# Sixteen of 24 modulation steps of the second layer in the even layer's last part, paced by product columns; ten small transfers of the odd layer on GpSimd's queue

## The chip, the core and the metric

The kernel runs on one core of a Trainium2 chip. The time is what the device takes for one execution, in microseconds (us). An execution on one core has a few engines that run side by side, each with its own queue of instructions: TensorE (PE, with PEld for its weight loads), VectorE (DVE), ScalarE (ACT), GpSimd (POOL) and SyncE (SP). SP computes nothing here; it issues DMA transfers. GpSimd issues some too. Engines wait for each other and for transfers by semaphores.

## The reference

A trunk of two layers over a prompt of 1024 tokens and 8 sample tokens (1032 columns in the kernel), width 1024. Each layer has a token mixer and an MLP, and each of these takes six vectors (shift, scale and gate, twice) from a small product of the condition `c` with a big matrix:

```python
for l in range(DEPTH):
    mod = jax.nn.silu(c) @ ada_w[l] + ada_b[l]      # (.., 1024) @ (1024, 6144)
    sh1, s1, g1, sh2, s2, g2 = split(mod, 6)
    h = rmsnorm(x, norm_mix[l]) * (1 + s1) + sh1
    x = x + g1 * mixer_l(h)        # l = 0: HGRN2 heads and gated short convolutions; l = 1: Mamba-2 (SSD)
    h = rmsnorm(x, norm_mlp[l]) * (1 + s2) + sh2
    x = x + g2 * (relu(h @ w1) ** 2 @ w2)
y = rmsnorm(x, norm_final)
```

(shortened: the prompt and the samples have their own `c`, nine columns together, and the mixers are not shown.) The matrix `ada_w[l]` is 1024 x 6144 in float32, 25.2 MB for each layer. Nothing but `c` goes in, so layer 1's `mod` can be computed at any time before layer 1 reads it.

The odd layer's mixer needs, for each half of the prompt, step sizes `dt` of 32 heads, their running sums times A, the exponentials of these, and for the sample tokens `dt` and `exp(dt*A)` spread to all channels of a head.

## The kernel before

The kernel goes through the program in stages, in this order: even layer (its last part about 350 to 512 us of the span, and a closing GEMM to 542), first MLP with a pass A to about 890 and a pass B to about 1270, odd layer to 2110, second MLP with pass A to 2437 and pass B to 2811. Products of float32 are made of three products of a rounded part and a remainder (`mm3`, lines 484, 487 and 488: high with high, high with low, low with high).

**Weights.** They come in units of 128 x 1024 on SP's queue (`raw<-W`), are rounded by ScalarE (`whi`) and the remainder is taken by VectorE (`wlo`). `need` takes the next unit from a list and prepares units up to three ahead (`AHEAD`). The transfers that SP issues stay in program order, so whatever stands in front of a weight tile on that queue, and waits, holds it up.

**Modulation.** `ada_gen(l, alloc, groups, depth)` is a generator. `groups` lists blocks of 512 columns by number (0 and 1 are the first shift, and so on to 11). One step is a quad: four products of 32 x 512 (line 316) that run side by side on quarters of the array, plus four loads of 256 KB each for the step `depth` ahead. A group of four blocks takes 8 quads, one of two blocks 4; then ScalarE copies the sums, TensorE transposes them (line 328) and VectorE adds the bias into `mod`. The accumulator stays taken from the group's first quad to the copy. `ada_steps(n)` makes n steps, and `need` calls it with `ada_rate`, one step for each weight unit.

**Where its steps stand before.** In the even layer's last part layer 0's groups (6, 7, 8, 9) and (10, 11) run, 12 quads, one for each weight unit. In the first MLP's pass B all 24 quads of layer 1 run, from unit 9 of 64 on, one for each unit. Pass B keeps four accumulators (`pd`) in PSUM, from which the modulation takes its own. Its units are the list `BOPS`; line 953 adds an accumulator, times a gate, into `x`, and the sample sums `racc` are added at line 960.

**Background.** `Background.tick` is called all through the layers and interleaves small pieces of mixer work with the products.

**The odd layer's step sizes.** For each half (hf 0 and hf 1) VectorE and ScalarE compute them, write them to DRAM and read them back spread over partitions. All of it goes by `dma`, that is by SP's queue in program order: running sums (`csd`) and their exponentials (`esd`) out; the last column out (`cdd`) and back as a 128 x 128 tile (`hs`, which must wait until `cdd` has landed); in the first half also the sample tokens' values out (`sd`, two transfers) and back as `dts` (four transfers). `dma_aux` does the same on GpSimd's queue, where the MLPs already issue theirs. In the listing the calls stand in the function that ends with `rest`.

Of the kernel before, what the change touches and what calls it, by code (L numbers as in the profile page):

```python
# [14 lines left out]
P = 128  # L15
# [3 lines left out]
NS = 8  # L19
# [112 lines left out]
class Background:  # L132


    def __init__(self):
        self.gens = []
        self.width, self.rate, self.due = 2, 1.0, 0.0

    def add(self, g, first=False):
        self.gens.insert(0 if first else len(self.gens), g)  # L140
        return g
# [4 lines left out]

    def tick(self, n=1):

        self.due += n * self.rate
        while self.due >= 1.0:  # L150
            self.due -= 1.0
            for g in self.gens[:self.width]:
                self.step(g)
# [8 lines left out]
def kernel(ctx: ExitStack, tc: tile.TileContext, A: dict):  # L162
# [53 lines left out]
    def dma(out, in_):  # L216
        ins = nc.sync.dma_start(out=out, in_=in_)
        if pinned_sp[0]:
            tc.keep_in_program_order(ins)

    def dma_aux(out, in_):

        tc.keep_in_program_order(nc.gpsimd.dma_start(out=out, in_=in_))

    bg = Background()
# [61 lines left out]
    def ada_gen(l, alloc, groups, depth=1, alloc2=None):  # L287
# [21 lines left out]
        for g, ch in enumerate(groups):  # L309
# [35 lines left out]
                V.tensor_add(out, pv[:, 1, :, :, 0:9], tmp)  # L345
            yield

    ada, ada_rate = [iter(())], [1]

    def ada_steps(n):  # L350
        for _ in range(n):
            next(ada[0], None)

    def mi(l, comp):
        return l * 48 + comp * 8
# [114 lines left out]
    def need(kind, idx):  # L470

        i = wpos[0]
        assert order[i] == (kind, idx), (i, order[i], kind, idx)
        wpos[0] += 1
        ada_steps(ada_rate[0])
        while len(units) <= min(i + AHEAD, max(i, limit[0] - 1)):
            units.append(prep(*order[len(units)]))
        u, units[i] = units[i], None
        return u

    def mm3(pt, trip, first=True, last=True):
        n = len(trip)
        for i, (wh, wl, xh, xl) in enumerate(trip):
            mm = PE.matmul(pt, wh, xh, start=first and i == 0, stop=False)  # L484
            if pinned[0]:
                tc.keep_in_program_order(mm)
            PE.matmul(pt, wh, xl, start=False, stop=False)  # L487
            PE.matmul(pt, wl, xh, start=False, stop=last and i == n - 1)  # L488
# [178 lines left out]
    def rows(units):  # L667

        return lambda m: [(hi[:, m * P:m * P + P], lo[:, m * P:m * P + P]) for hi, lo in units]
# [108 lines left out]
    def mlp(l, gi, finish, more=None):  # L778
# [77 lines left out]
        for i, (p, q) in enumerate(AOPS):  # L856
            n = APOS[p, q]
# [70 lines left out]
        for n, (i, hb, q, mp) in enumerate(BOPS):  # L928
            j = n % 8
            hi, lo = need(f"b{l}", n)  # L930
            if n == 8 and more:
                ada[0] = more()
            elif i == 6 and hb == 0 and j == 0:
                ada_steps(99)
            rh, rl = R[i, q // 2]
            seq = BSEQ if i else BFIRST
            qs = [qq for qq, mm in seq if mm == mp]
            for m in (2 * mp, 2 * mp + 1):
                if q == qs[0]:
                    pts[m] = pd()  # L940
                pt = pts[m]
                for b in range(2) if hb is None else (hb,):
                    c = slice(b * hw, b * hw + hw)
                    mm3(pt[:, b, 0:hw], [(hi[:, o:o + P], lo[:, o:o + P], rh[:, k, c], rl[:, k, c])
                                         for k, o in ((q % 2 * 4 + k, 256 * k + m % 2 * P) for k in range(4))],
                        q == qs[0], q == qs[-1])
                if q == qs[-1]:
                    for o, th in BOUT[BPROD[i]]:
                        mt = 4 * o + m
                        gate = mod[:, gi + mt, 0:1]  # L950
                        if hb is None:
                            xv = v2(x[:, mt, th * HX:th * HX + HX])
                            V.scalar_tensor_tensor(xv, pt[:, :, 0:hw], gate, xv, op0=ALU.mult, op1=ALU.add)  # L953
                        else:
                            xv = x[:, mt, th * HX + hb * hw:th * HX + hb * hw + hw]
                            V.scalar_tensor_tensor(xv, pt[:, hb, 0:hw], gate, xv, op0=ALU.mult, op1=ALU.add)
                        if hb != 1:
                            sv = pt[:, 0, 0:4] if th else pt[:, 1, hw - 4:hw]
                            av = acc[:, mt, 4 * th:4 * th + 4]
                            V.tensor_add(av, sv, av)  # L960

            if i == 0:
                split_op((2, 2, 2, 2, 0, 1, 2, 1)[j])
            else:
                split_op((0, 0, 1, 1, 1, 1, 0, 1)[j] if i == 1 else (2, 1, 1, 1, 1, 1, 0, 1)[j] if i < 6 else (2, 1, 0, 0, 0, 0, 0, 0)[j] if hb == 0 else 0)
            if j == (5 if i else 3) and i < 6:
                load_op(i + 1, 1)
            elif j == 7 and i < 5:
                load_op(i + 2, 0)

            if i == 6 and j == 7 and hb == 0:
                V.tensor_mul(acc, acc, mod[:, gi:gi + KT, 1:9])
                for k in FOURS:
                    V.tensor_add(x[:, k, 512:520], acc[:, k], xs[:, k])
            if i >= 5:
                next(fin, None)
            bg.tick()
# [316 lines left out]
    def even_mixer(res, last, rest):  # L1294
        hgrn_consts()
        V.tensor_scalar(gnh, vec("gn"), -0.5, None, op0=ALU.mult)
        dma(scs, A["st_sc"])
        fa = [new_ff(), new_ff()]
        g01 = head(0, fa[0], rest, fa[1])
        g01 += head(1, fa[1])  # L1300
        fb = [new_ff(), new_ff()]
        g23 = head(2, fb[0])
        bg.drain(*g01)
        out_seq(rows([need("eo", 0), need("eo", 1)]), [ff_src(f) for f in fa], res)
        g23 += head(3, fb[1])
        c0 = conv_uv(0)
        c1 = conv_uv(1)
        bg.drain(*g23)
        ada_steps(99)
        turn = [0]  # L1310

        def alloc(w):
            turn[0] += 1
            return t2(w) if turn[0] % 2 else t3(w)
        ada[0] = ada_gen(0, alloc, ((6, 7, 8, 9), (10, 11)))
        out_seq(rows([need("eo", 2), need("eo", 3)]), [ff_src(f) for f in fb], res)
        fa = [new_ff(), new_ff()]
        unit_gemm(need("e", 16), (0, 1, 2), conv_gate(c0, fa[0]))
        unit_gemm(need("e", 17), (0, 1, 2), conv_gate(c1, fa[1]))
        c0 = conv_uv(2)  # L1320
        c1 = conv_uv(3)
        out_seq(rows([need("eo", 4), need("eo", 5)]), [ff_src(f) for f in fa], res)
        fa = [new_ff(), new_ff()]
        u0, u1 = need("e", 18), need("e", 19)
        for b in range(3):
            unit_gemm(u0, (b,), conv_gate(c0, fa[0]))
            unit_gemm(u1, (b,), conv_gate(c1, fa[1]))
        bg.width = 1
        ws = rows([need("eo", 6), need("eo", 7)])
        ada_steps(99)  # L1330
        out_last(ws, [ff_src(f) for f in fa], res, (3, 2), last, (2,))
        dma(A["o_scp"], scp_o)
        dma(A["o_scs"], scs)
# [12 lines left out]
    def odd_dt(hf, o):  # L1346

        u = need("dt", 0)
        nt = 128 if hf else 136
# [13 lines left out]
        e, q, z = dtile(nt), dtile(nt), dtile(nt)  # L1363
# [11 lines left out]
        dtt = z  # L1375
# [7 lines left out]
        ecs = e[:, 0:P]  # L1383
# [2 lines left out]
        dma(esd, ecs)  # L1386

        cdd = dr.tile([P, 1], F32, name="cdd", tag="cdd", bufs=2)
        dma(cdd, ecs[:, P - 1:P])
        o.cd = hs3[:, 3]  # L1390
        dma(o.cd, cdd.rearrange("(o p) a -> o (p a)", o=1).broadcast_to([P, P]))

        dl = q[:, 0:P]
        act(dl, cs[:, 0:P], AF.Exp, bias=cs[:, P - 1:P], scale=-1.0)
# [1 line left out]
        if hf == 0:  # L1396

            sd = dr.tile([2, 32, NS], F32, name="sd")
            es = sm(8)
            act(es, da[:, P:nt], AF.Exp)  # L1400
            dma(sd[0], dtt[0:32, P:nt])
            dma(sd[1], es[0:32])
            o.dts = ph.pool.tile([P, 2, 16, NS], F32, name="dts")
            for q in range(2):
                sv = sd[q].rearrange("(m h) b -> h m b", h=2)
                for hh in range(2):
                    dma(o.dts[64 * hh:64 * hh + 64, q], sv[hh:hh + 1].broadcast_to([64, 16, NS]))

        def rest():
            yield  # L1410
# [485 lines left out]
    with ExitStack() as e:  # L1896
        phase(e, "mlp0", n3=N3M)
        psum(e, "mlp0", 0, 0, 4)
        upto("mlp0")
        turn = [0]  # L1900

        def alloc(w):
            turn[0] += 1
            return t2(w) if turn[0] % 2 else t3(w)
        mlp(0, mi(0, 5), to_odd, more=lambda: ada_gen(1, alloc, ((0, 1, 2, 3), (4, 5, 6, 7), (8, 9, 10, 11))))
        M["tags"] = "hB", "hA"
        bg.drain(*bg.gens)

# [190 lines left out]
```

## Time and profile before

| | us |
|---|---|
| median of three runs | 2817.61 |
| lowest, highest | 2815.24, 2818.54 |
| the profiled execution | 2820.48 |
| its span, first to last instruction | 2818.7 |
| its mean granted TensorE clock | 0.977 |

The profile is of one execution, which took 2820.48 us, 2.87 more than the median of the runs. How to read what is quoted below: rows of windows give busy time and instructions of each engine in a stretch of the span; rows of grouped instructions give line, engine, operation and tile, count, then busy us, mean ns of one, and idle time before them with what ended it. Rows of waits give the waiting engine with its tile and line, what ended the wait, and total us, count and longest. Rows of the timeline give start, duration, engine, line, operation and tile, and in brackets how long the engine had stood idle and what ended that. SPq and POOLq are the queues' own instructions.

### The profile page before, as it was taken

The page shows a single profiled execution, that of the slowest core. Times are in us where ns is not written, and L with a number is a line of the kernel's source. Part 1 is how long each engine was busy: PE and PEld are TensorE (multiplying, and loading weights), DVE is VectorE, ACT ScalarE, POOL GpSimd, SP SyncE. Part 2 cuts the span into 40 slices and gives each one's busy share as a digit, 9 for nine tenths or more (in the row PEclk, how much of TensorE's full clock was granted, in tenths as well). Part 3 has the DMA queues.
Part 4 walks back from the last instruction along what each step waited for, and adds up shares of the span by engine and source line. Part 5 has one row for each costly group of instructions (what it writes and reads, how often), then busy time and mean ns, then how long its engine had stood idle before and what let it go on. Part 6 is the DMA issues. An engine that isn't in the chain of part 4 may idle for free. (4 is left out here: it accounts for less than half of the span.)

```text
span 2818.7 us, 49673 instructions
## 1 busy us (share of the span) xinstructions
PE 2662.7 (94%) x19442; PEld 2453.6 (87%) x19442; DVE 1995.6 (71%) x3800; ACT 1496.6 (53%) x2477; POOL 277.9 (10%) x476
## 2 busy tenths in 40 slices
PE   6999999999999989998899999999999999999897
PEld 4889888899999878988799897787789999999897
DVE  5666444787765566765788888998778776667766
ACT  5785411564444333346686776878666444434233
POOL 0000000023214110000000000000001321311010
PEclk8999999999999999999999999999999999999999
DMA  8232333256539899744655545533334644879754
GB/s 299 76 106 65 103 120 119 89 194 228 172 126 347 307 373 390 260 150 100 157 149 129 183 125 153 146 124 113 117 124 154 237 161 152 286 277 360 267 182 150
DMA packets 215066, 519.33 MB, mean 184 GB/s; under 512 B 38000, under 2 KB 55792, under 8 KB 214832
## 3 DMA queue, kind: packets, MB, share of 16 engines
q1 hardware_dynamic: 167728, 353.16, 39.7%
q0 software_dynamic: 47104, 163.00, 15.9%
q8 instruction: 153, 2.51, 0.4%
q14 instruction: 81, 0.66, 0.1%
HBM read 404.38 MB, written 111.68 MB: 183 GB/s over the span
## 5 line engine op out<-in xcount | busy, mean ns | idle before, releaser
L484 PE MATMUL pg<-hh,whi 128*128 128x256 f32 (+2 forms) x1616 | 536.5, 332 | 14.3 <-ACT xy L1434 7.2
L484 PE MATMUL pd<-rr,whi 128*128 128x258 f32 x1792 | 516.3, 288 | 11.7 <-DVE racc L960 8.8
L487 PE MATMUL pg<-hl,whi 128*128 128x256 f32 (+2 forms) x1616 | 523.6, 324 | 1.9 <-DVE hl L587 1.9
L488 PE MATMUL pd<-rr,wlo 128*128 128x258 f32 x1792 | 512.4, 286 | 13.4 <-DVE wlo L454 10.5
L488 PE MATMUL pg<-hh,wlo 128*128 128x256 f32 (+2 forms) x1616 | 522.9, 324 | 0.0
L487 PE MATMUL pd<-rr,whi 128*128 128x258 f32 x1792 | 511.2, 285 | 0.0
L464 DVE TENSOR_TENSOR wlo<-raw,whi 128x1024 fp32r<-128x1024 f32 x222 | 270.7, 1221 | 203.0 <-ACT whi L463 193.4
L463 ACT CAST whi<-raw 128x1024 fp32r<-128x1024 f32 x222 | 231.5, 1044 | 329.0 <-PE pg L487 202.3
L484 PEld LDWEIGHTS pd<-rr,whi 128*128 128x128 f32 x1792 | 344.5, 192 | 32.1 <-issue 26.0
L488 PEld LDWEIGHTS pd<-rr,wlo 128*128 128x128 f32 x1792 | 344.4, 192 | 16.3 <-DVE wlo L454 11.1
L484 PEld LDWEIGHTS pg<-hh,whi 128*128 128x128 f32 x1616 | 309.0, 191 | 51.4 <-issue 8.9
L487 PEld LDWEIGHTS pd<-rr,whi 128*128 128x128 f32 x1792 | 344.2, 192 | 0.5 <-issue 0.5
L487 PEld LDWEIGHTS pg<-hl,whi 128*128 128x128 f32 x1616 | 308.9, 191 | 30.6 <-issue 5.2
L488 PEld LDWEIGHTS pg<-hh,wlo 128*128 128x128 f32 x1616 | 308.4, 191 | 24.1 <-issue 0.4
L484 PE MATMUL pd<-hh,whi 128*128 128x258 f32 x1024 | 294.9, 288 | 21.6 <-ACT whi L424 10.6
L487 PE MATMUL pd<-hh,whi 128*128 128x258 f32 x1024 | 293.2, 286 | 1.0 <-DVE hh L688 1.0
L488 PE MATMUL pd<-hh,wlo 128*128 128x258 f32 x1024 | 291.8, 285 | 0.0
L484 PEld LDWEIGHTS pd<-hh,whi 128*128 128x128 f32 x1024 | 197.3, 193 | 24.9 <-ACT whi L424 11.0
L836 ACT CAST rr<-rr 128x1032 fp32r<-128x1032 f32 x112 | 117.3, 1056 | 156.5 <-DMA rr<-td 156.4
L487 PEld LDWEIGHTS pd<-hh,whi 128*128 128x128 f32 x1024 | 197.1, 192 | 2.2 <-DVE hh L688 1.7
L488 PEld LDWEIGHTS pd<-hh,wlo 128*128 128x128 f32 x1024 | 197.3, 193 | 0.0
L837 DVE TENSOR_TENSOR rr<-rr 128x1032 fp32r<-128x1032 f32 x112 | 135.5, 1227 | 64.4 <-ACT rr L836 64.1
(335 smaller groups left out, 5844.2 us busy)
## 6 DMA issues: line engine op xcount, KB each, us to landing
raw<-W SPq DMA_DIRECT2D x371, 512.0 KB, 4.3
td<-x POOLq DMA_DIRECT2D x224, 258.0 KB, 3.9
rr<-td POOLq DMA_DIRECT2D x112, 516.0 KB, 8.4
t<-ada SPq DMA_DIRECT2D x192, 256.0 KB, 5.7
t<-W SPq DMA_DIRECT2D x64, 256.0 KB, 6.0
sd<-t SPq DMA_DIRECT2D x64, 256.0 KB, 5.8
t<-sd SPq DMA_DIRECT2D x64, 256.0 KB, 5.9
t<-csd SPq DMA_DIRECT2D x64, 256.0 KB, 4.8
```

Of the source, the lines that this page charges most:

```text
L463: S.copy(hi, raw)
L464: V.tensor_sub(lo, raw, hi.bitcast(F32))
L484: mm = PE.matmul(pt, wh, xh, start=first and i == 0, stop=False)
L487: PE.matmul(pt, wh, xl, start=False, stop=False)
L488: PE.matmul(pt, wl, xh, start=False, stop=last and i == n - 1)
L836: S.copy(hi[:, c:c + 2], src)
L837: V.tensor_sub(lo[:, c:c + 2], src, hi[:, c:c + 2].bitcast(F32))
```

## The change

It has two parts. First, layer 1's groups (0, 1, 2, 3) and (4, 5, 6, 7), 16 quads, are made in the even layer's last part, behind layer 0's 12 quads; loads go two steps ahead there. The pace is no longer one step for each weight unit: `mm3` counts the columns of the products it issues, and `tick` makes a step for every 8200 columns. Pass B of the first MLP keeps the group (8, 9, 10, 11), 8 quads, one for every fourth unit. Second, `cdd`, `hs`, `sd` and `dts` of the odd layer go by GpSimd's queue.

```diff
@@ Background
         self.width, self.rate, self.due = 2, 1.0, 0.0
+        self.between = None
...
     def tick(self, n=1):
 
+        if self.between:
+            self.between()
         self.due += n * self.rate
@@ ada_gen and what drives it
     ada, ada_rate = [iter(())], [1]
+    cols, ada_cols = [0, 0], 8200
+
+    def ada_between():
+        while cols[0] >= cols[1]:
+            cols[1] += ada_cols
+            ada_steps(1)
...
     def mm3(pt, trip, first=True, last=True):
         n = len(trip)
+        cols[0] += 3 * n * trip[0][2].shape[-1]
@@ the MLP's pass B
                 ada[0] = more()
             elif i == 6 and hb == 0 and j == 0:
                 ada_steps(99)
+            elif n % 4 == 0:
+                ada_steps(1)
@@ the even layer's last part
-        ada[0] = ada_gen(0, alloc, ((6, 7, 8, 9), (10, 11)))
+
+        def gens():
+            yield from ada_gen(0, alloc, ((6, 7, 8, 9), (10, 11)), 2)
+            yield from ada_gen(1, alloc, ((0, 1, 2, 3), (4, 5, 6, 7)), 2)
+        ada[0], ada_rate[0] = gens(), 0
+        cols[1], bg.between = cols[0], ada_between
...
         bg.width = 1
+        bg.between = None
         ws = rows([need("eo", 6), need("eo", 7)])
         ada_steps(99)
@@ the odd layer's step sizes
-        dma(cdd, ecs[:, P - 1:P])
+        dma_aux(cdd, ecs[:, P - 1:P])
         o.cd = hs3[:, 3]
-        dma(o.cd, cdd.rearrange("(o p) a -> o (p a)", o=1).broadcast_to([P, P]))
+        dma_aux(o.cd, cdd.rearrange("(o p) a -> o (p a)", o=1).broadcast_to([P, P]))
...
-            dma(sd[0], dtt[0:32, P:nt])
-            dma(sd[1], es[0:32])
+            dma_aux(sd[0], dtt[0:32, P:nt])
+            dma_aux(sd[1], es[0:32])
...
-                    dma(o.dts[64 * hh:64 * hh + 64, q], sv[hh:hh + 1].broadcast_to([64, 16, NS]))
+                    dma_aux(o.dts[64 * hh:64 * hh + 64, q], sv[hh:hh + 1].broadcast_to([64, 16, NS]))
@@ the first MLP's call
-        mlp(0, mi(0, 5), to_odd, more=lambda: ada_gen(1, alloc, ((0, 1, 2, 3), (4, 5, 6, 7), (8, 9, 10, 11))))
+        mlp(0, mi(0, 5), to_odd, more=lambda: ada_gen(1, alloc, ((8, 9, 10, 11),)))
```

How this moves instructions is read from the order in which each engine's queue holds them. First SP's queue in the even layer's last part; `t<-ada` is a load of 256 KB for a quad, `raw<-W` a weight unit. Before:

```order
L217 DMA t_3928<-ada 128x512
L217 DMA t_3930<-ada 128x512
L217 DMA raw<-W 128x1024 x2
L217 DMA t_4042<-ada 128x512
L217 DMA t_4044<-ada 128x512
L217 DMA raw<-W 128x1024
L217 DMA t_4138<-ada 128x512
L217 DMA t_4140<-ada 128x512
L217 DMA raw<-W 128x1024
```

The same place now:

```order
L220 DMA t_3759<-ada 128x512
L220 DMA t_3797<-ada 128x512
L220 DMA t_3756<-ada 128x512
L220 DMA t_3758<-ada 128x512
L220 DMA t_3799<-ada 128x512
L220 DMA t_3879<-ada 128x512
L220 DMA t_3796<-ada 128x512
L220 DMA t_3798<-ada 128x512
L220 DMA raw<-W 128x1024 x2
```

More loads of the modulation now stand between two weight units. On TensorE's queue in this part the quads stood 72 product rows apart and stand 24 to 48 rows apart now, 28 in all, the last transposes ahead of the closing GEMM; in pass B they stood 49 rows apart, one in each unit, and now 193.

Second, SP's queue in the odd layer's first half, from the running sums on. Before:

```order
L217 DMA csd<-dtr 128x128
L217 DMA esd<-dtr 128x128
L217 DMA cdd<-dtr 128x1
L217 DMA sd<-dtr 32x8
L217 DMA sd<-sm 32x8
L217 DMA hs_13231<-cdd 128x128
L217 DMA bcd<-bcz 128x8x1
L217 DMA dts<-sd 64x16x8 x4
L217 DMA raw<-W 128x1024
L217 DMA t_13842<-csd 128x512
L217 DMA t_13844<-csd 128x512
```

SP's queue there now:

```order
L220 DMA csd<-dtr 128x128
L220 DMA esd<-dtr 128x128
L220 DMA bcd<-bcz 128x8x1
L220 DMA raw<-W 128x1024
L220 DMA t_13842<-csd 128x512
L220 DMA t_13844<-csd 128x512
```

And GpSimd's queue now, from the last loads of the first MLP to both halves of the odd layer:

```order
L226 DMA rr<-td 128x2x516 x48
L226 DMA cdd<-dtr 128x1
L226 DMA hs_13231<-cdd 128x128
L226 DMA sd<-dtr 32x8
L226 DMA sd<-sm 32x8
L226 DMA dts<-sd 64x16x8 x4
L226 DMA cdd<-dtr 128x1
L226 DMA hs_18160<-cdd 128x128
```

The transfers that SP issued between `esd` and the weight tile, apart from `bcd`, have gone to GpSimd's queue in another order: there `hs`, which waits for `cdd`, now stands ahead of `sd` and `dts`.

Third, SP's queue at the same step of the second half. Before:

```order
L217 DMA cdd<-dtr 128x1
L217 DMA t_18441<-csd 128x512
L217 DMA raw<-W 128x1024
L217 DMA hs_18160<-cdd 128x128
L217 DMA t_18500<-st_ss 128x512
```

Now:

```order
L220 DMA esd<-dtr 128x128
L220 DMA raw<-W 128x1024
L220 DMA t_18441<-csd 128x512
L220 DMA t_18500<-st_ss 128x512
L220 DMA raw<-W 128x1024
```

Here `cdd` and `hs` have gone, and the load of a recurrent state, `st_ss`, no longer stands behind `hs`.

## The prediction

> **What bounds the kernel now.** I read the head of the page first: it says which engine is full.
>
> ```profile
> span 2818.7 us, 49673 instructions
> PE 2662.7 (94%) x19442; PEld 2453.6 (87%) x19442; DVE 1995.6 (71%) x3800; ACT 1496.6 (53%) x2477; POOL 277.9 (10%) x476
> ```
>
> TensorE works for 2662.7 of 2818.7 us, so 156 us is all that better order can win; the rest is products, and the change takes none away. Next I read busy time in windows around each place the change touches: the even layer's last part, the part of the first MLP's pass B that holds layer 1's modulation, the fullest 50 us in it, and the like part of the second MLP, which has no modulation.
>
> ```profile
> core 0: us, PE busy (x) PEld busy (x) DVE busy (x) ACT busy (x) POOL busy (x), PEclk, DMA share, GB/s
> 350.00:512.00 162.00, 162.00 (x1035) 136.36 (x1037) 70.22 (x144) 27.07 (x42) 0.00 (x0) 1.00 0.33 108
> 930.00:1215.00 285.00, 271.70 (x2197) 246.79 (x2197) 189.96 (x303) 99.73 (x132) 28.21 (x40) 0.99 0.88 321
> 1050.00:1100.00 50.00, 46.62 (x366) 40.50 (x359) 30.11 (x53) 11.30 (x17) 3.66 (x6) 0.97 1.03 388
> 2492.00:2752.00 260.00, 247.35 (x1993) 246.51 (x1993) 187.56 (x295) 97.30 (x130) 28.21 (x40) 0.96 0.72 255
> ```
>
> The place the work goes to is full on TensorE (162.00 of 162.00) and light on DMA (0.33). The place it leaves is heavy on DMA (0.88, in its middle 1.03), but TensorE idles there for 13.3 us only. Without modulation the second MLP idles as long: 12.7 us. That comparison decides how much the heavy traffic costs.
>
> **The modulation steps.** Layer 1's 24 steps ("quads": four products of 32x512, each in two passes, so 8 records) become 8 in pass B and 16 in the even layer's tail.
>
> ```profile
> L316 PE MATMUL pd<-t,ct 128*32 128x512 f32 x192 | 25.7, 607 | 3.0 <-DMA t<-ada 3.0
> L328 PE MATMUL psm<-cm,t 128*128 128x128 f32 x4 | 0.6, 272 | 0.0
> ```
>
> 192 records are 24 quads in 25.7 us, 1.07 us each. Sixteen cost 17.1 us, and their two groups of transposes 2 x 0.6 = 1.2 (the second row is one group in the tail). TensorE is full in the tail and nearly so in pass B, so this is +18.3 there and −18.3 here: **net 0**. The products before the even layer's closing GEMM suffice for 36 steps (297,000 columns over 8200) where 34 are needed, and the order has the last step ahead of that GEMM, so there is no lump at its end.
>
> The new stage could have waits that the old one hadn't. TensorE is busy throughout 350–512 with 12 quads; with 28, and loads of 1 MB each in front of the weights on SP's queue, the DMA has to move 16.8 MB more. Spread over 162 us that is 104 GB/s on top of 108, well under the 388 that a row above shows. Cover is the two steps of lookahead and the two or so units by which the weights run ahead. A load that has to wait for its buffer also holds the weight tiles queued behind it on SP. If the cover fails at places, each costs a load's wait like the 3.0 us over 4 places below; I take **+1**, with 0 and +5 as ends.
>
> For what pass B gives back, the waits of TensorE there, and in the second MLP:
>
> ```profile
> PE pd L484 <- DVE racc L960: 8.8, 4, 3.2
> PE pd L316 <- DMA t<-ada: 3.0, 4, 1.9
> PE pd L488 <- DVE wlo L454: 10.5, 3, 4.0
> ```
>
> The first two rows are the first MLP's. The 3.0 on modulation loads goes by two thirds: **−2.0**. The 8.8 is TensorE waiting for VectorE to empty an accumulator. A group of quads holds one of the four accumulators while it is open: before from unit 10 to 36 of 64, after from 16 to 48. It is held about as long in both, so I change nothing, **0**, with −8.8 (all gone) and +8.8 (doubled, where the new hours are worse) as ends. The third row is the second MLP's: with no quads to fill a unit, TensorE catches up with the weight split, 10.5 in three stalls. Three of four units of the first MLP now have no quad either, but its clock and traffic differ; I take a little under a third, **+3**, with 0 and +10.5 as ends. How alike the two places are is seen from the evacuations:
>
> ```profile
> L953 DVE SCALAR_TENSOR_TENSOR x<-pd,mod,x x52: 740/744/754, 932.9 to 1213.2; 128x516 f32<-128x516 f32 x52
> ...
> L953 DVE SCALAR_TENSOR_TENSOR x<-pd,mod,x x52: 740/745/756, 2494.9 to 2750.4; 128x516 f32<-128x516 f32 x52
> ```
>
> The same 52 evacuations take 280.3 us with quads and 255.5 without. The difference, 24.8, is nearly the 25.7 us of quads. So quads cost what they compute, and traffic at a share of 0.88 against 0.72 cost nothing beyond it. Pass B together: **+1**.
>
> The Trainium skill speaks for more. "DMA: Bandwidth & Descriptors", section "Where 436 GB/s comes from", puts HBM's limit for one core near 358 GB/s and says that it binds transfers between HBM and SBUF; by it 16.8 MB would be some 47 us (an estimate from that page) of a full path that leaves pass B. The window 1050–1100 moved 388, above that limit, so here it didn't bind as stated; by the rule the relief below would be the likeliest case.
>
> **The odd layer's small transfers.** They leave SP's queue for GpSimd's. SP around the first one:
>
> ```profile
> 1289.14 0.43 SPq L217 DMA_DIRECT2D cdd<-dtr  x1
> ...
> 1296.35 0.34 SPq L217 DMA_DIRECT2D hs<-cdd  x1
> 1296.78 0.38 SPq L217 DMA_DIRECT2D bcd<-bcz  x1
> 1297.26 11.26 SPq L217 DMA_DIRECT2D dts<-sd  x4
> 1308.57 0.82 SPq L217 DMA_DIRECT2D raw<-W  x1
> 1309.43 0.91 SPq L217 DMA_DIRECT2D t<-csd  x2
> ```
>
> SP waits from some 1290.5 (two sd are left out) to 1296.35 for cdd to land before hs may read it, then spends 11.26 us on issuing four dts. Behind them stand a weight tile and the decays t<-csd, which ScalarE and then TensorE want:
>
> ```profile
> 1315.50 0.40 ACT L1520 ACTIVATE t<-t,hs 128x128 f32<-128x128 f32 x1 [10.92 <-DMA t<-csd]
> PE pg L484 <- ACT xy L1434: 7.2, 1, 7.2
> PE psm L1536 <- DVE t L1524: 5.0, 2, 3.1
> PE psm L1536 <- DVE t L1528: 4.7, 1, 4.7
> PE psm L1545 <- DVE mxs L1446: 2.0, 1, 2.0
> PE psm L1517 <- ACT xy L281: 1.3, 1, 1.3
> ```
>
> With bcd and csd issued up to 18 us earlier, ScalarE's 10.92 goes, and TensorE's 7.2 on xy, which stands behind that activation in ScalarE's queue: **−7**, ends 0 and −7.2. What is late next is VectorE:
>
> ```profile
> 1309.61 0.17 DVE L1596 TENSOR_TENSOR dx<-dts,xy 128x8 f32<-128x8 f32 x1 [5.15 <-DMA dts<-sd]
> 1316.86 1.23 DVE L464 TENSOR_TENSOR wlo<-raw,whi 128x1024 fp32r<-128x1024 f32 x1 [7.09 <-ACT whi L463]
> vd<-t POOLq DMA_DIRECT2D x4, 4.0 KB, 10.5
> dts<-sd SPq DMA_DIRECT2D x4, 32.0 KB, 11.5
> L223 POOL DMA_DIRECT2D vd<-t x4: 899/901/901, 64.2 to 274.2; - x4
> ```
>
> On GpSimd's queue nothing else follows until the second MLP, so a wait there for cdd holds up only hs, sd and dts. VectorE waits for dts itself. No row shows dts from GpSimd's queue; the nearest is vd, 0.90 to issue and 10.5 to land. On POOL dts is still behind hs, which waits for cdd: three issues (hs and two sd) and the four dts are 7 x 0.90 = 6.3 from 1296.35, and with 10.5 the last lands at about 1313; the first, which dx needs, at about 1310.5. Ends: 1306 (if issue overlaps landing) and past 1320 (if broadcasts of 32 KB cost GpSimd the 2.8 each that SP shows). VectorE's next work in the old order resumed at 1316.86 only, so some 4 us of cover lie behind it; I count no loss. The 5.0, 4.7, 2.0 and 1.3 that follow have to do with VectorE's own queue, and I let them stand.
>
> The Trainium skill has a rule against this term: the same page, section "Issuing engines are not separate DMA queues", says that issuing from several engines only saves the sequencer's time to initiate, "usually small relative to the DMA itself". Here the row has 11.26 us for it, as long as the 11.5 to land; by the rule this term would fall away and the "same" case below be the likeliest.
>
> The second time (no dts; only cdd and hs move):
>
> ```profile
> 1698.48 0.42 SPq L217 DMA_DIRECT2D cdd<-dtr  x1
> 1706.35 0.32 SPq L217 DMA_DIRECT2D hs<-cdd  x1
> 1706.76 0.38 SPq L217 DMA_DIRECT2D t<-st_ss  x1
> 1711.94 0.40 ACT L1604 ACTIVATE t<-t,dts 128x128 f32<-128x128 f32 x1 [3.53 <-DMA t<-st_ss]
> PE psm L1498 <- DVE hs L1417: 2.2, 1, 2.2
> PE psm L1536 <- ACT t L1604: 1.2, 1, 1.2
> PE psm L1504 <- DVE ssd_state L1554: 0.9, 1, 0.9
> ```
>
> The state load st_ss waits behind hs, and ScalarE 3.53 for it. TensorE's small waits here are 4.3 together; **−2.5**, between 0 and −4.3.
>
> **Sum.** 0 + 1 + 1 − 7 − 2.5 = −7.5, against the profiled execution's 2820.48 (span 2818.7 and 1.8 around it): 2813.0. That execution stands 2.9 above the median of the three runs, 2817.61, so on the median's footing it is **2810.1**.
>
> **Rivals.**
> - *Relief.* Less traffic in pass B frees the accumulator waits (−8.8) and the weight split (no +3), and the odd layer's later waits shrink by a few us: about −20, 2797. For it: DMA at 1.03 in the middle. Against: 280.3 − 255.5 equals the quads.
> - *GpSimd too late.* Its issues of dts cost as much as SP's, dts lands after 1317, VectorE's dx takes over what ScalarE waited for, and the odd terms vanish: +2, 2819.6. For it: no row of such a transfer on that queue; cdd still gates it. Against: 0.90 an issue.
> - *A bare load chain (the slower side).* A unit of pass B is 48 products, by the second MLP's window 48 x 247.35/1993 = 6.0 us of TensorE, with a quad 7.0; if load and split of its weights need longer than 6.0, TensorE catches up in three units of four. Then the second MLP's 10.5 appears in full and the accumulator waits double: +10.5 + 8.8 − 2 + 1 − 9.5 = +8.8, 2826.4. It decides where the chain is longer than a unit without quad. For it: the 10.5 exists there; against: only three stalls in 52 units.
> - *It doesn't do what it says*: steps pile up before the closing GEMM, or transfers land no earlier. The order speaks against the first; change near nothing, 2817.6.
>
> **How the numbers follow.** Forecast 0.50, about −13 to −3; relief 0.16; GpSimd too late 0.17; load chain 0.14; not as said 0.03. A measurement tells 0.2% from no change, 5.6 us. Of the forecast seven parts in ten lie beyond it: faster is 0.35 + 0.16 = 0.51; same is 0.15 + 0.17 + 0.03 = 0.35; slower 0.14. Each unknown at its worse end alone (the split +7.5, the accumulators +8.8, the loads +4, the odd terms +9.5) leaves at most 2819.6, at its better end at least 2801.3. The range is 2797 to 2823: it holds the forecast, half of relief and the cases near no change, and leaves out 0.08 below and most of the 0.14 above, about 2 in 10.
>
> **What would show it.** Right: TensorE in the even tail still without idle time and some 18 us longer; pass B shorter by 17 to 19; the 10.92 on csd gone and xy's 7.2 with it; dts landed before 1317 (less the shift). Wrong: waits on t<-ada or raw in the tail above 5 us; waits on racc or wlo in pass B above 15; dx waiting for dts while TensorE waits on VectorE; a second half of the odd layer no shorter.

## The result and the profile after

The changed kernel is **slower**: a median of 2836.65 us (2826.23 to 2841.95, 7 runs) against 2815.86 us of seven runs of the kernel before, a ratio of 1.0071 with a 95% interval of 1.0055 to 1.0086. That is some 20 us; the prediction had 2810.1 and a range up to 2823. The profiled execution is the fastest of the seven, 2826.23 us, so it shows where time is lost, but less of it than the median.

The head of its page, and busy time in windows at the places of the two first windows of before, moved with the program:

```profile
span 2824.3 us, 49710 instructions
PE 2664.7 (94%) x19442; PEld 2453.2 (87%) x19442; DVE 1995.4 (71%) x3800; ACT 1496.0 (53%) x2477; POOL 285.4 (10%) x486
```

```profile
core 0: us, PE busy (x) PEld busy (x) DVE busy (x) ACT busy (x) POOL busy (x), PEclk, DMA share, GB/s
350.00:532.00 182.00, 182.00 (x1174) 138.98 (x1173) 71.37 (x149) 28.07 (x44) 0.00 (x0) 1.00 0.55 186
940.00:1226.00 286.00, 268.28 (x2144) 258.95 (x2143) 193.51 (x303) 101.87 (x134) 30.76 (x44) 0.96 0.78 278
```

The engines do the same work. The tail takes its 16 steps without a gap (182.00 of 182.00), as forecast, at a DMA share of 0.55 where it was 0.33. In pass B the share has fallen from 0.88 to 0.78, but TensorE's idle time has grown, from 13.3 us to 17.7. Its waits there, and the groups of quads and transposes in the tail:

```profile
PE pd L495 <- DVE racc L973: 11.4, 4, 5.3
PE pd L331 <- ACT t L326: 4.9, 1, 4.9
PE pd L499 <- DVE wlo L474: 1.0, 1, 1.0
```

```profile
L319 PE MATMUL psm<-t,ct 128*32 128x512 f32 x224 | 30.3, 603 | 0.0
L331 PE MATMUL psm<-cm,t 128*128 128x128 f32 x16 | 2.5, 276 | 0.0
```

A new wait stands in the second row: the transposes of the last group (line 331) wait 4.9 us for its copy on ScalarE. The waits for the accumulator went from 8.8 to 11.4 instead of staying; the 3.0 us on modulation loads are gone. In the odd layer's first half, GpSimd's timeline, VectorE's row for dts and TensorE's longest wait in that stretch:

```profile
1299.27 0.56 POOL L226 DMA_DIRECT2D cdd<-dtr  x1 [91.81 <-ACT dtr L284]
1307.70 0.55 POOL L226 DMA_DIRECT2D hs<-cdd  x1 [7.87 <-DMA cdd<-dtr]
1308.24 0.53 POOL L226 DMA_DIRECT2D sd<-dtr  x1
1308.76 0.50 POOL L226 DMA_DIRECT2D sd<-sm  x1
1322.15 3.29 POOL L226 DMA_DIRECT2D dts<-sd  x4 [12.89 <-DMA sd<-dtr]
```

```profile
1335.12 0.17 DVE L1615 TENSOR_TENSOR dx<-dts,xy 128x8 f32<-128x8 f32 x1 [20.30 <-DMA dts<-sd]
```

```profile
PE pg L499 <- DVE wlo L474: 10.2, 1, 10.2
```

Three landings follow each other on one queue: hs waits for cdd, sd is issued behind hs, dts waits for sd. VectorE's dx stood 5.15 us for dts before and stands 20.30 now, with the split of the next weights behind it, and TensorE waits 10.2 for that split.

What the prediction hoped for came in part. The decays csd, ScalarE's wait for them and TensorE's for xy:

```profile
1307.40 0.80 SPq L220 DMA_DIRECT2D t<-csd  x2
1320.68 0.40 ACT L1539 ACTIVATE t<-t,hs 128x128 f32<-128x128 f32 x1 [5.73 <-DMA t<-csd]
PE pg L495 <- ACT xy L1453: 2.3, 1, 2.3
```

The program stands 10 us later here than before, so csd left some 12 us earlier; but it took 14.3 us to land where it had taken 6.2, and ScalarE's 10.92 became 5.73 and TensorE's 7.2 became 2.3.

**Stretch by stretch.** To place the difference, each product of a trace was matched with the same product of the first profile of before (by tile, form and occurrence, without the quads), and the change of its start time was taken: what a stretch adds is the difference between its two ends. The stretches are bounded in the time of before: 340–562 is the tail, 890–1172 most of pass B, 1172–1283 its end and the way to the odd layer, 1283–1400 the odd layer's first heads. In us, with the ratio of the timed runs beside it, and all the runs of the next section:

```
                      tail  pass B  its end  odd first  elsewhere   ratio, 95%
                   340-562 890-1172 -1283    1283-1400
after                +21.4   -19.8    +6.8     +4.9       -7.9    1.0071  1.0055-1.0086
after_again          +21.1   -18.4    +6.8    +10.9      +10.3    1.0077  1.0060-1.0093
before_again          -0.2    +1.0    +2.2     +0.3       +7.3    0.9998  0.9982-1.0015
transfers_only         0.0    -0.3    +0.8    +10.0       +6.9    1.0065  1.0043-1.0087
transfers_again       -0.1    -0.2    +0.4     +8.1       +3.1    1.0045  1.0030-1.0061
sd_ahead_of_hs       +21.0   -16.8    +4.9     -3.3      +13.5    1.0051  1.0032-1.0071
out_sp_back_pool      -0.2    -0.6    +1.8     +0.2       +3.2    0.9994  0.9978-1.0009
dts_in_rows           +0.2    +2.7    +0.7     +0.2       +0.3    1.0003  0.9990-1.0016
rows_back_pool        +0.6    -0.7    +1.0     -1.9      +10.3    0.9999  0.9982-1.0015
steps_only           +21.0   -15.8    +6.0     +0.2       +8.8    1.0036  1.0022-1.0050
early_group          +21.1   -16.4    -0.1    +10.8      +10.6    1.0068  1.0045-1.0091
copy_at_44           +21.3   -13.9    +1.3     +0.3      +16.2    1.0049  1.0031-1.0067
all_in_tail          +33.9   -26.7    +0.6     +0.2       +1.7    1.0031  1.0017-1.0045
bcd_in_rows           -0.1    -2.0    +1.9    -14.1       +7.0    0.9954  0.9937-0.9971
bcd_and_dts_in_rows   +0.5    -1.9    -0.4    -17.9      +10.5    0.9945  0.9927-0.9963
transfers_bcd_rows    -0.2    +4.4    -0.7    -16.4       +5.0    0.9948  0.9927-0.9968
change_bcd_rows      +21.0   -19.4    +5.8    -15.2      +14.1    0.9995  0.9983-1.0006
```

The four named stretches are steady from profile to profile. "Elsewhere", all other stretches together, is not: it is +7.3 for the unchanged kernel itself. In the change the first two leave +2 to +3, the end of pass B another +7, and the odd stretch +5 to +11.

### The profile page after: what moved, and what is told of

The parts are those of the page before. It is cut to its first block, busy times and chain, and to the rows that moved or that the text cites. A ratio compares the mean times of both kernels' runs of the same rounds, so it can differ in the third digit from the quotient of the medians.

```text
span 2824.3 us, 49710 instructions
## 1 busy us (share of the span) xinstructions
PE 2664.7 (94%) x19442; PEld 2453.2 (87%) x19442; DVE 1995.4 (71%) x3800; ACT 1496.0 (53%) x2477; POOL 285.4 (10%) x486
## 5 line engine op out<-in xcount | busy, mean ns | idle before, releaser
L499 PE MATMUL pg<-hh,wlo 128*128 128x256 f32 (+2 forms) x1616 | 522.3, 323 | 10.2 <-DVE wlo L474 10.2
L495 PE MATMUL pd<-rr,whi 128*128 128x258 f32 x1792 | 517.7, 289 | 13.2 <-DVE racc L973 11.4
L499 PEld LDWEIGHTS pd<-rr,wlo 128*128 128x128 f32 x1792 | 346.7, 193 | 11.5 <-DVE wlo L464 9.2
L499 PEld LDWEIGHTS pg<-hh,wlo 128*128 128x128 f32 x1616 | 307.2, 190 | 34.6 <-DVE wlo L474 10.4
L495 PE MATMUL pd<-hh,whi 128*128 128x258 f32 x1024 | 295.1, 288 | 24.3 <-ACT whi L434 10.5
L495 PEld LDWEIGHTS pd<-hh,whi 128*128 128x128 f32 x1024 | 197.6, 193 | 27.6 <-ACT whi L434 10.9
```

## The experiments

They ran later, beside runs of the kernel before with medians of 2827 to 2828 us, so ratios are to be compared and not times. The edits are shown shortened. The repeat of the kernel before sets the scatter:

> The kernel before, unchanged, for the scatter of its stages between executions. Every theory: ratio 1.000 within 0.2%; stretches outside the three places of the change differ from the first profile by up to 6 us either way, those at the three places (350 to 560, 890 to 1283, 1283 to 1400) by less than 3.

Ratio 0.9998 (0.9982 to 1.0015). The stretches of the change moved by at most 2.2 us, the others by 7.3 together. A difference below 3 us in a stretch, or 0.2% in a ratio, means nothing here.

**Each part alone.**

```diff
 transfers_only, transfers_again: the kernel before, with
-        dma(cdd, ...); dma(o.cd, ...); dma(sd[0], ...); dma(sd[1], ...); dma(o.dts[...], ...)
+        dma_aux(cdd, ...); dma_aux(o.cd, ...); dma_aux(sd[0], ...); dma_aux(sd[1], ...); dma_aux(o.dts[...], ...)
 steps_only: the changed kernel, with
-        dma_aux(...)     # these ten
+        dma(...)
```

> Only the second part of the change: cdd, hs, sd and dts on GpSimd's queue, all 24 modulation steps where they were before. Theory 1 (sd waits its turn behind hs on the new queue, so dts lands some 10 us later than before and VectorE's dx holds the weight split behind it): 3 to 8 us slower than before, VectorE waits about 20 us for dts, TensorE waits about 10 us once for the split. Rival, the prediction's own term (SP's queue comes free earlier, dts in time): 7 to 10 us faster than before, and the whole loss of the change comes from the modulation steps.

> Only the first part of the change: 16 steps in the even layer's last part, 8 in pass B, the odd layer's small transfers on SP's queue as before. Theory 2 (pass B gives back less than the tail takes, because the last group's copy and transposes now stand at the end of the pass, where ScalarE is late, 4.9 us, and the accumulator waits do not shrink): 6 to 14 us slower than before. Rival (the steps are neutral and the loss is in the odd layer's transfers or comes from a lower clock that any dense stretch brings): within 4 us of before.

The transfers alone cost 1.0065, the steps alone 1.0036: both lose. Their costs together, 29 us, or 23 with the repeat below, are somewhat above the change's 20 to 22 us, by about as much as the intervals allow. The rival in which the transfers gain 7 to 10 us fell. In transfers_only VectorE waits 22.4 us for dts and TensorE 12.5 for the split, and the stretch is 10.0 longer. The two repeats:

> transfers_only once more. Its first profile was of the fastest of its six runs, with 10 us in the stretch 1283 to 1400 where the ratio had 18. Theory 1 with a landing that varies (sd and dts on GpSimd's queue): that stretch between 8 and 18 us here, ratio 1.004 to 1.007. Rival (the transfers cost something elsewhere too): the stretch stays at 10 and another one, in the odd layer or the second MLP, is 5 us or more longer than in both profiles of before.

> The changed kernel, unchanged, on this chip and with a second profile. Both theories 1 and 2 together: 1.006 to 1.010 of before; against before_again the tail 21 us longer, pass B and its end 12 to 15 shorter, 1283 to 1400 5 to 12 longer. If the 10 us by which the first profile stood under the median of its runs came from these stretches, they are longer here; if from elsewhere, they are the same.

The stretch came out at 8.1 and 10.9, the ratios at 1.0045 and 1.0077, so the 4.9 of the change's first profile belongs to an execution 10.4 us below the median of its runs. The ratios of the transfers alone, 13 to 18 us, are still 5 to 8 us more than the stretch shows. Their profiled executions lay 5.8 and 7.8 us below the medians, so scatter between executions can hold that much; no other stretch carries it steadily, and where it comes from stays open.

**The steps: what pass B gives back.**

```diff
 early_group (the changed kernel), pass B
-            elif n % 4 == 0:
+            elif 8 < n < 19:
                 ada_steps(1)
 copy_at_44 (steps_only)
                 ada[0] = more()
+                ada_steps(1)
 all_in_tail (steps_only)
-    ada_cols = 8200,  tail: groups (0, 1, 2, 3), (4, 5, 6, 7),  pass B: (8, 9, 10, 11)
+    ada_cols = 6500,  tail: groups (0, 1, 2, 3), (4, 5, 6, 7), (8, 9, 10, 11),  pass B: none
```

> The changed kernel, but pass B's 8 steps one for each unit from unit 9 on (as the old pace) instead of every fourth unit, so that the group's copy and transposes stand at unit 18 and not at 48. Theory 2: the 4.9 us in which TensorE waits for the copy go, accumulator waits fall below 11.4 as the accumulator is held 9 units and not 32: 5 to 10 us faster than the changed kernel. Rival (the wait at the pass's end is taken over by the norm that is late there anyway, 2.1 before): 0 to 3 us faster.

> As steps_only, but pass B's eight steps start one call earlier, so that the group's copy and transposes stand at unit 44, four units ahead of the pass's closing half, and not at 48; the pace stays one step for every fourth unit. Theory 2a (the copy at 48 is late because ScalarE's queue holds the next norm's work ahead of it): the 4.9 us at the copy go and the stretch 1172 to 1283 gives back 4 to 6 us of the 6 lost; accumulator waits unchanged at 11 to 13; 3 to 6 us faster than steps_only. Rival (any copy in this pass costs that, as the accumulator is needed): the wait moves to unit 44 and nothing is won.

> As steps_only, but all 24 steps of layer 1 in the even layer's last part (a step for every 6500 columns), none in pass B. Theory 3 (a step costs its 1.2 us wherever it stands; what pass B loses in accumulator waits it gets back as waits for the weight split, since every unit is bare): the tail 31 us longer than before, pass B and its end together 28 to 35 us shorter, waits for the split 10 to 15 us as in the second MLP, waits for the accumulator under 3; total from 4 us faster to 4 us slower than before. Rival (relief): pass B 40 us shorter, since the traffic goes, and the kernel 8 to 12 us faster than before.

In early_group and copy_at_44 the wait for the copy is gone, and the end of pass B, between +5 and +7 with it, falls to −0.1 and +1.3: the place of the copy was its cause. On the changed kernel's ScalarE it stood last behind the next norm's work, which waits for the last additions into `x`:

```profile
1216.20 0.63 ACT L562 ACTIVATE t<-x 128x512 f32<-128x512 f32 x1 [0.72 <-DVE x L966]
1216.73 1.03 ACT L473 CAST whi<-raw 128x1024 fp32r<-128x1024 f32 x1
1218.67 0.63 ACT L562 ACTIVATE t<-x 128x512 f32<-128x512 f32 x1 [0.91 <-DVE x L966]
1219.21 0.57 ACT L326 COPY t<-pd 128x512 f32<-128x512 f32 x1
```

But the kernels were no faster for it: 1.0068 against the change's 1.0071 to 1.0077, and 1.0049 against 1.0036 of steps_only, intervals that overlap. The expected 5 to 10 and 3 to 6 us were not seen in the times. For early_group a row shows where part of it went; its waits in pass B, and those of all_in_tail:

```profile
PE pd L499 <- DVE wlo L464: 11.4, 5, 5.3
...
PE pd L495 <- DVE racc L973: 1.8, 1, 1.8
```

```profile
PE pd L499 <- DVE wlo L464: 12.5, 4, 5.2
```

Where a stretch of units has no quad, TensorE catches up with the weight split, 11.4 and 12.5 us, as the second MLP did with 10.5; where a group stays open, it waits for the accumulator, 11.4 to 13.5. One wait takes the other's place: 12.5 without steps for 8.8 and 3.0 with all of them. So pass B gives back 26.7 us for 24 steps, no more than their 25.7 of work and 1.8 of transposes, and relief by less traffic is refuted. The tail takes 33.9 for the same 24, so theory 3 missed as well: it had the kernel within 4 us of before, and 1.0031 is 9. Its quads in all_in_tail, 36 in 38.4 us:

```profile
L319 PE MATMUL psm<-t,ct 128*32 128x512 f32 x288 | 38.4, 603 | 2.5 <-DMA t<-ada 2.5
```

They compute 1.07 each there too, and one load came 2.5 late. The rest of the difference, 3 to 4 us, is spread in small slips, most of them of 0.1 us at the first product behind a quad; what makes them was not tried. A lower clock, part of the rival to theory 2, is not the cause there: the tail's granted clock is 1.00 before and after. In pass B it went from 0.99 to 0.96; the products there (`pd<-rr`) took 288.0 ns on average against 285.5 before, but 287.3 in before_again, so this is within the scatter.

**The transfers: place in the queue, issue, or pieces.**

```diff
 sd_ahead_of_hs (the changed kernel), first half
-    cdd, hs, sd, sd, dts x4      # GpSimd's queue
+    cdd, sd, sd, hs, dts x4
 out_sp_back_pool (the kernel before)
-    dma(o.dts[...], ...), dma(o.cd, ...)
+    dma_aux(o.dts[...], ...), then dma_aux(o.cd, ...)      # cdd and sd stay on SP's queue
 dts_in_rows (the kernel before), rows_back_pool (out_sp_back_pool)
-            dma(sd[0], dtt[0:32, P:nt])
+            dma(sd[0, hh], dtt[hh:32:2, P:nt])      # for hh in 0, 1; sd[1] likewise
-                    ... sv[hh:hh + 1].broadcast_to([64, 16, NS]))
+                    ... sd[q, hh] as one row of 128 .broadcast_to([64, 16 * NS]))
```

> The changed kernel, but on GpSimd's queue sd is issued ahead of hs (cdd, sd, sd, hs, dts instead of cdd, hs, sd, sd, dts). Theory 1: sd leaves some 8 us earlier, dts is issued about 9 us earlier, VectorE's wait for dts falls from 20.3 to about 11, TensorE's 10.2 on the split to 1 to 3, and the kernel is 6 to 9 us faster than the changed one. Rival (the issue and landing of such transfers on GpSimd's queue is what is slow, wherever they stand): less than 3 us.

The stretch, between +5 and +11 in the change, fell to −3.3: with sd out of the wait for cdd, dts was issued 9.1 us after sd instead of 13.9, and TensorE's wait for the split fell to 0.2. The place in the queue was a cause. The ratio, 1.0051, is only 0.2 to 0.3% below the change's, with intervals that overlap, and not below that of steps_only.

> The kernel before, all 24 modulation steps where they were; of the odd layer's small transfers only those that read back (dts and hs) go by GpSimd's queue, dts ahead of hs, while cdd and sd go out by SP's queue as before. Theory 1 (what matters is that no transfer stands behind one that waits for a landing; SP's sd lands in some 7 us, and SP then needn't issue dts): in the stretch 1283 to 1400 about 7 us less than before, VectorE's dx waits no longer than the 5 us of before, and the whole kernel is 4 to 9 us faster than before. Rival (a broadcast transfer on GpSimd's queue lands too late anyway, 12 to 15 us after its issue): no change, within 3 us.

> The kernel before, with all transfers on SP's queue and all steps in place, but the sample tokens' values are written to DRAM already sorted (sd in four transfers of 16 heads), so that each dts reads back 64 x 128 numbers in whole rows of 512 bytes and not 64 x 16 pieces of 32 bytes. Theory 4 (what holds SP and delays the landing is the 1024 small pieces of each dts, 11 us of issue and 11 to land): SP issues dts in under 3 us, the decays csd leave some 8 us earlier, VectorE's wait for dts is under 2 us, the stretch 1283 to 1400 is 5 to 9 us shorter than before and the kernel 5 to 9 us faster. Rival (SP is held by hs, which waits for cdd to land, and the stretch by VectorE and ScalarE's own work): less than 3 us.

> As dts_in_rows, but dts and hs go back by GpSimd's queue, like in out_sp_back_pool. Theory 4: the landing of dts there falls from 16 us to 4 to 7, and the stretch 1283 to 1400 gives 5 to 10 us against before; the same as dts_in_rows within 4 us. Rival (GpSimd's queue lands a broadcast late whatever its pieces are): dts lands 10 us or more after its issue, the stretch gives less than 3 us.

All three free SP's queue, and none gains anything: 0.9994, 1.0003, 0.9999. Here the prediction's main term is tested by itself. SP and ScalarE in dts_in_rows:

```profile
1302.11 2.40 SPq L217 DMA_DIRECT2D dts<-sd  x4
1304.55 0.58 SPq L217 DMA_DIRECT2D raw<-W  x1
1305.18 1.10 SPq L217 DMA_DIRECT2D bcd<-bcz  x1
1306.33 1.29 SPq L217 DMA_DIRECT2D t<-csd  x2
1320.73 0.40 ACT L1521 ACTIVATE t<-t,hs 128x128 f32<-128x128 f32 x1 [10.97 <-DMA t<-csd]
```

dts is issued in 2.40 us instead of 11.26, and csd 4.7 us after hs instead of 13.1; ScalarE waits 10.97 for it as it did before, 10.92. An earlier issue gave no earlier landing here (csd took 14.3 us to land, 6.2 before), and in the change only part of one. In out_sp_back_pool, dts likewise:

```profile
1307.04 3.28 POOL L223 DMA_DIRECT2D dts<-sd  x4 [97.30 <-DMA sd<-sm]
1323.99 0.17 DVE L1596 TENSOR_TENSOR dx<-dts,xy 128x8 f32<-128x8 f32 x1 [11.07 <-DMA dts<-sd]
```

Cheap to issue, 0.82 each, and seventeen us until VectorE has it; whole rows instead of small pieces made that 14.8 (rows_back_pool). So the transfers were held after their issue. What was issued ahead of them, of csd in dts_in_rows and of dts in the two others, is `bcd`, the eight samples' values of one group, written to DRAM transposed, 4 KB in 1024 pieces of 4 bytes. In dts_in_rows dts itself stood ahead of `bcd`, and landed in 4.2 to 4.4 us.

```diff
 bcd_in_rows (the kernel before), bcd_and_dts_in_rows (dts_in_rows),
 transfers_bcd_rows (transfers_only), change_bcd_rows (the changed kernel)
-            d = dr.tile([NS, P], F32, name="bcd", tag="bcd", bufs=4)
-            dma(d.rearrange("b p -> p b"), o.bcz[:, par + i, 512:520])
+            d = dr.tile([2, P, 4], F32, name="bcd", tag="bcd", bufs=4)
+            for q in range(2):
+                dma(d[q], o.bcz[:, par + i, 512 + 4 * q:516 + 4 * q])
...
-                dma(t, ds[i][4 * q:4 * q + 4] ...)    # read back, and bc[i][:, c] of it
+                dma(t, ds[i][q] ...)                  # read back, and every fourth element of it
```

> The kernel before, but the two bcd transfers of each group, which write 4 KB in 1024 pieces of 4 bytes, are written in four transfers of 128 pieces of 16 bytes, and read back in that order. Theory 5 (these pieces keep the DMA engines busy while next to nothing moves, and every transfer behind them, dts and csd above all, lands 12 to 20 us after its issue): what is issued behind bcd lands in 4 to 9 us, the stretch 1283 to 1400 is 2 to 6 us shorter, dts still in small pieces; the kernel 2 to 7 us faster than before. Rival (dts's own 4096 pieces are what clogs): less than 2 us.

> The kernel before with both: bcd in pieces of 16 bytes and dts in rows of 512. Theory 5: csd lands within 6 us of its issue at about 1306, ScalarE's wait for it falls from 11 to under 4, TensorE's 7 on xy goes, the stretch 1283 to 1400 is 5 to 9 us shorter and the kernel 5 to 10 us faster than before. Rival (the stretch is bound by something else, as dts_in_rows gave nothing): within 3 us.

> transfers_only with bcd in pieces of 16 bytes. Theory 5: sd lands in 8 to 9 us where it took 13 to 19, dts in 9 or less, VectorE's wait for dts falls from 22 to 12 to 16, the stretch 1283 to 1400 is 1 to 6 us longer than before where it was 8 to 10; ratio 1.000 to 1.003. Theory 1 alone (only the place behind hs counts): the stretch stays 7 to 10 us longer, ratio 1.004 or more.

> The changed kernel with bcd in pieces of 16 bytes. Theory 5: as with transfers_bcd_rows the stretch 1283 to 1400 loses 4 to 9 us of its 5 to 11, the tail and pass B are untouched (21 longer, 12 to 15 shorter); ratio 1.003 to 1.005. Theory 1 alone: 1.006 to 1.009 as in after_again.

The first three went further than expected, and the fourth as well: it came out at 0.9995. The kernel before gained 0.46% by it (0.9954, 0.9937 to 0.9971), and the stretch lost 14.1 us. What bcd does to the DMA engines is plainest without dts's pieces: 22 us from 2 us ahead of the first bcd, in 40 slices (busy tenths, GB/s, packets), in dts_in_rows and in bcd_and_dts_in_rows:

```profile
DMA  0014496998639454254719893744598994310022
GB/s 0 0 42 117 131 235 182 305 205 211 76 57 34 11 4 7 7 11 19 19 7 34 22 30 7 19 11 56 93 231 320 370 215 113 61 1 0 0 52 67
DMA packets 3137, 1.86 MB, mean 85 GB/s; under 512 B 2224, under 2 KB 2608, under 8 KB 3136
```

```profile
DMA  0013297899937048988764200057962000000004
GB/s 0 0 35 93 70 235 167 237 334 164 83 31 30 4 89 179 212 223 336 278 250 173 40 0 0 0 97 194 357 268 67 0 0 0 0 0 0 0 0 52
DMA packets 1769, 2.36 MB, mean 107 GB/s; under 512 B 736, under 2 KB 1120, under 8 KB 1767
```

In the first the engines are about half busy at 4 to 34 GB/s through 15 slices, 8 us (from the 13th on); the csd and the weights that stand behind come through only after that, at 93 to 370 GB/s. The packets in the trace show what is busy there. The 4-byte packets of the first bcd are over by 1310 us and took some 9 ns each; from 1310 to 1318 there are 58 packets of csd, 2 KB each, of 1.4 us on average, and in the 3 us after that 133 of 0.14 us each. So the pieces don't fill the engines themselves; what comes right behind them is slow, and why is not shown. In the second the gap is three slices, and csd follows at 89 to 336. The second bcd of dts_in_rows landed after 20.9 us; for this stretch of bcd_and_dts_in_rows no landing of bcd is on record, and in bcd_in_rows they landed in 3.2 to 5.9. In bcd_and_dts_in_rows csd landed in 7.2 to 7.4 us instead of 14.3, and ScalarE's wait for it is down to

```profile
1316.05 0.40 ACT L1521 ACTIVATE t<-t,hs 128x128 f32<-128x128 f32 x1 [3.88 <-DMA t<-csd]
```

and the ratio is 0.9945. And the transfers of the change, on GpSimd's queue and in the change's own order, with bcd in rows:

```profile
1304.70 0.55 POOL L223 DMA_DIRECT2D hs<-cdd  x1 [8.81 <-DMA cdd<-dtr]
1305.24 0.53 POOL L223 DMA_DIRECT2D sd<-dtr  x1
1305.76 0.50 POOL L223 DMA_DIRECT2D sd<-sm  x1
1311.44 3.28 POOL L223 DMA_DIRECT2D dts<-sd  x4 [5.19 <-DMA sd<-dtr]
```

sd now lands in 6 us and not in 13 to 20, and the loss of the transfers is gone: 0.9948 (0.9927 to 0.9968) with them moved, 0.9954 without. Nor is it a gain: the stretch differs by 2.3 us, less than counts here. Theory 1 alone, which counted only the place in the queue, had 1.004 or more. The change with bcd in rows stands at 0.9995, that is 0.0047 above the same kernel without the moved steps, near the steps' own price of 0.0036.

The Trainium skill names such transfers: "DMA: Bandwidth & Descriptors", section "Rules for kernel authors", says that a last dimension that isn't contiguous comes down to one descriptor for each element, and to rearrange it. The traces agree: between 1295 and 1345 us there are 2692 packets of 4 bytes before, and in bcd_in_rows 512, with 512 of 16 bytes; the one rearrangement made 0.9954.

**Versions that beat both kernels:** bcd_and_dts_in_rows (0.9945), transfers_bcd_rows (0.9948) and bcd_in_rows (0.9954), which the intervals don't tell apart. None moves a modulation step.

## Why the prediction was wrong

- **"ScalarE's 10.92 goes, and TensorE's 7.2 on xy … −7": this step failed.** It took an earlier issue for an earlier landing. csd left some 8 us earlier in dts_in_rows, and ScalarE waited as long; in the change it left some 12 us earlier, and ScalarE's wait only halved, to 5.73, while TensorE's 7.2 became 2.3 and a new 10.2 for the split outweighed it. The profile of before had a sign of it: dts of 32 KB took 11.5 us to land behind bcd, and the second bcd 15.2. The time was there to be had, and more, but not by moving transfers: −14 to −18 in the stretch with bcd in rows, whether they move or not.
- **"three issues (hs and two sd) and the four dts are 7 x 0.90 = 6.3": this step failed too.** It counted issues only; dts reads what sd wrote, so the landing of sd belongs in between. On SP sd had been issued ahead of the wait for cdd; on GpSimd's queue it came behind. Instead of at about 1310.5 the first dts reached VectorE at 1335.12, in an execution shifted by some 10 us there, and the stretch cost 5 to 11 us where −7 was forecast. The rival "GpSimd too late" had the right wait, VectorE's dx, and put it at +2 overall. The second half's −2.5 did not come either: TensorE's waits for `hs` (2.2) and `ssd_state` (0.9) stayed.
- **"net 0" and pass B's +1: mis-sized.** The steps were forecast at +2 in all (0, +1 for loads in the tail, +1 in pass B) and cost some 10 (1.0036). No load was late in the tail, and the quads took 1.08 us each as against 1.07; but 16 quads and their transposes cost 21 us there against 18.3 forecast, some 2 of it in the small slips, and pass B with its end gave back 10 to 14 us, not the 17.3 forecast.
- **"It is held about as long in both, so I change nothing" was mis-sized.** The accumulator waits went from 8.8 to 11.4 and 13.4, inside the bounds given, and the open group ended at the pass's end, where its copy found ScalarE late: +4.9 that had no term.
- **"+3" for the weight split was too much here.** With a quad in every fourth unit the wait was 1.0; with none it was 12.5. The slower rival, a bare load chain, thus had the right sign with a mechanism that this kernel doesn't show.
- **The relief rival is refuted** by all_in_tail. The rule on issuing engines that the prediction weighed (the Trainium skill's "DMA: Bandwidth & Descriptors", section "Issuing engines are not separate DMA queues") fits these runs: three kernels that only freed SP's queue or moved reads to GpSimd's stand within 0.1% of before. By that rule the odd term was zero and the case "same" the likeliest, and the loss by the transfers came from the order of the queue and from the pieces, which it doesn't speak of.

The whole: steps +10 us (1.0036), transfers +13 to +18 (1.0045 to 1.0065, of which the odd stretch shows 8 to 10), both measured together +20 to +22, where −7.5 was forecast.

## What to carry to other kernels

Before a transfer is moved to free a queue, look at its landing time and at what the DMA engines move meanwhile: engines that were busy at a few GB/s pointed here to small pieces ahead of it, and an earlier issue then mostly waited longer. A chain of transfers through DRAM costs a landing for each link, so on an in-order queue whatever starts another chain goes ahead of the first wait. And work that is taken out of a stretch doesn't take the stretch's waits along: here another wait of the same size came in their place, and the work cost its full time, or more, where it went.

## What the runs showed of the hardware

A long wait of TensorE cost more than itself. Windows of transfers_only around its 12.5 us:

```profile
1310.00:1320.00 10.00, 8.20 (x69) 8.00 (x68) 0.00 (x0) 4.79 (x10) 0.00 (x0) 1.00 0.53 132
1320.00:1325.00 5.00, 0.84 (x7) 0.59 (x5) 0.00 (x0) 2.09 (x3) 2.85 (x4) 0.77 0.13 1
1325.00:1330.00 5.00, 0.00 (x0) 0.00 (x0) 0.00 (x0) 0.00 (x0) 0.43 (x1) 0.50 0.82 12
1330.00:1335.00 5.00, 1.61 (x7) 1.61 (x8) 3.02 (x7) 0.00 (x0) 0.00 (x0) 0.50 0.24 34
1335.00:1340.00 5.00, 5.00 (x40) 5.00 (x39) 3.68 (x10) 4.21 (x10) 0.00 (x0) 0.87 0.29 101
```

The granted clock (the third number from the end) falls to 0.50 in the wait, still is 0.50 while the first products run, 7 in 1.61 us, and 0.87 in the 5 us after. Eight products of one kind, from 1310 to 1320 us and from 1330 to 1340:

```profile
L488 PE MATMUL pg<-hh,wlo 128*128 128x256 f32 x8 | 2.2, 281 | 0.0
L488 PE MATMUL pg<-hh,wlo 128*128 128x256 f32 x8 | 3.0, 381 | 12.5 <-DVE wlo L464 12.5
```

One takes 281 ns ahead of the wait and 381 behind it. Also unexpected: 4 KB in 1024 pieces of 4 bytes delayed what came behind them (csd, sd and dts), while the four dts, 4096 pieces of 32 bytes, landed in 4.7 to 6.9 us in bcd_in_rows, once those were gone, and in 9.4 to 12.1 before.
